# Output projection as seven products of halves, with weight sums made by adding transfers in DRAM

## The chip, the cores and the metric

The kernel runs on one core of one Trainium2 chip. The metric is the device time of one execution, in microseconds. The kernel before takes 1063.2 us (median of three runs, 1063.05 to 1063.6). A core has a matrix engine (TensorE, PE in the profile, with its weight loads as PEld), a vector engine (VectorE, DVE), a scalar engine (ScalarE, ACT), a general engine (GpSimd, POOL) and a queue engine (SyncE, SP) that here only starts transfers. Each engine works through its own instructions in order, and waits on semaphores for the others.

## The reference

One layer of an encoder block on 1024 tokens with 1024 channels, all float32:

```python
h = rms_norm(x, norm1_g)
a, gate, q, k, v = split(h @ w_in)               # 512 columns each
conv_out = silu(layer_norm(depthwise_conv_31(a * sigmoid(gate)) + bias))
q, k = rms_norm per head of 64
attn_out = neighbourhood_attention(q, k, v, rpb) # 16 rows x 64 columns of tokens, window 8 x 16
x = x + concat([conv_out, attn_out]) @ w_out     # output projection, 1024 x 1024 x 1024
h = rms_norm(x, norm2_g)                         # the second norm
x = x + (silu(h @ w_gate) * (h @ w_up)) @ w_down # 2816 hidden channels
```

## The kernel before, in words

**Precision.** Each float32 operand of a large product is split into a high part (a cast to fp32r on ACT) and a low part (the rest, a subtraction on DVE or POOL): `split`, lines L104 (cast) and L108 (subtraction). One block product is then three matmuls with 512 columns, high by high, high by low, low by high: `mac`, L112, L113, L114. Weights come by SP into raw buffers of 512 KB (three of them, pool R), and `take` splits the next one, cast on ACT, subtraction on POOL, and asks for a later one.

**Order.** The order of the work on each engine is the order in which the program issues it. Small work is put between the block products of TensorE by hand: functions are appended to the list `woven`, and `weave`, called after each `mac`, runs the next one.

**Stages.** First the k projection, the gated convolution input, the q projection (`project(0, t)`, eight token tiles) and the values (`value(t)`, eight tiles). Beside the last two run the convolution: its taps are DVE's (L319) but for some taps that ACT multiplies (L344) and POOL adds up (L345), and DVE joins the two per channel block (L324). The raw blocks of the value weights, w20 to w23, are split between the q projections. SP meanwhile builds the bias tables of the attention in DRAM (L487) and loads them (L588). Then the attention: 32 steps, each with scores (L615), a softmax whose maximum and sum run on DVE (L628) and ACT (L630) and whose scaling runs on POOL (L637), transposes (L646) and the product with the values (L662). Results of eight groups of tokens are split into high and low parts (`evac_hi` L669, `evac_lo` L674).

**Output projection.** Eight row tiles of 128 tokens by two halves of 512 output columns, each over eight blocks of 128 channels (four of the attention, four of the convolution). Column half 0 is tiles `pj`, half 1 tiles `pk`. Between the block products of `pj` lie the transposes of the convolution result (`conv_T`, L728), its statistics (`conv_stats`, L735 to L737, `conv_scale`, L747 to L756) and the transposes and silu of the normed rows (`conv_silu`, L761, L762). `resid` (L775) adds a finished tile to x on DVE.

**Second norm and gate products.** Between the block products of `pk` the rows are normed (`norm2`, L857 to L861, `norm2_out`, L867). The gate and up products, and the down product, already are made of seven products of halves each, where the four quadrants of both operands are combined by sums and differences and only seven of eight block products are made. Operands A11 and A12 are 32 transposes (`t2_one`, L994); the five others, S1 to S4 and A22, are sums of rows (`s_sum`, L944) that are transposed each by itself, 16 transposes each (`s_T`, L963), woven between the first products. Sums of the gate weights are made by `t_sums` on DVE (L893). `prep` splits the next weight operand ahead of its product, and `product` and `evac` run the products (m1 to m7) and combine their results.

**Buffers.** In SBUF 22 tiles of 4 KB per partition (G), 3 raw ones (R), 6 of 16 KB (H), 5 small ones (st). In PSUM four banks `mm`, two `tp` and one pair `cv`.

## Time and profile before

| | |
|---|---|
| median of three runs | 1063.2 us (1063.05 to 1063.6) |
| the profiled execution | 1064.03 us |
| its span, first to last instruction | 1062.2 us |
| mean granted TensorE clock | 0.999 of full speed |
| TensorE, DVE, ACT, POOL busy | 98%, 66%, 42%, 37% of the span |
| moved by transfers | 144.05 MB, 136 GB/s on average |

How to read the lines that follow: a row of the timeline has its start in microseconds from the start of the span, its length, the engine, the line of the program, the operation, output and inputs, their shapes and how many instructions are merged in it; in square brackets the idle time of the engine before it and who ended it. A row of the waits names the waiting engine and line, then whom it waited for, then the total, the number and the longest. A row of the chain of waits has a start, a length and the piece of work that the end of the run hung on. A row of the groups has the busy time in all, the mean length of one in nanoseconds and the idle time before. A row of the windows gives, for a stretch of time, the busy time of PE, PEld, DVE, ACT and POOL with the count of instructions, then the clock, the share of the transfer engines that was busy, and GB/s. Matmuls overlap, so the length of one (0.39 us) is more than the distance from one to the next.

### The profile page before, as it was taken

Reading aid. Unit: us, or ns where it says so; the run is one execution under the profiler, and the core shown is the slowest. Engines: PE = TensorE matmul, PEld = TensorE weight load, DVE = VectorE, ACT = ScalarE, POOL = GpSimd, SP = SyncE. Lnnn points to the kernel's source line nnn. Section 1 sums busy time; section 2 is a strip of 40 time slices with the busy share of each in tenths; the row PEclk is TensorE's granted clock in tenths of the full one; section 3 lists DMA queues with packets and bytes.
Section 4 is the critical chain, followed back from the end, with each engine's and each line's share of the span. In section 5 each row is a group of like instructions: output and inputs, shape, how many; then the busy total and the mean of one; then the engine's idle time right before and its main releaser. Section 6 shows DMA issues by size and latency. Waiting matters only on the chain.

```text
span 1062.2 us, 13969 instructions
## 1 busy us (share of the span) xinstructions
PE 1045.4 (98%) x5068; PEld 847.3 (80%) x5068; DVE 699.8 (66%) x1072; ACT 443.7 (42%) x874; POOL 397.3 (37%) x308
## 2 busy tenths in 40 slices
PE   7999999999999999999999999999999999999997
PEld 5788888776667888788888888888888888888886
DVE  6768998966765247666565564564655567858883
ACT  6456346626776334532323223332233344433441
POOL 0126568823542301444554544545454200002310
PEclk9999999999999999999999999999999999999999
DMA  9416681245504412032322222232132597634641
GB/s 333 164 47 225 217 257 36 75 161 154 165 34 161 136 80 99 21 129 77 136 91 104 109 99 95 104 129 100 70 131 78 194 322 276 209 99 132 205 127 43
DMA packets 68244, 144.05 MB, mean 136 GB/s; under 512 B 12496, under 2 KB 21200, under 8 KB 67536
## 3 DMA queue, kind: packets, MB, share of 16 engines
q1 hardware_dynamic: 66336, 139.95, 38.3%
q10 hardware_dynamic: 1840, 3.22, 0.9%
q8 instruction: 40, 0.66, 0.3%
q14 instruction: 28, 0.23, 0.1%
HBM read 103.99 MB, written 44.76 MB: 140 GB/s over the span
## 4 chain that ended last, share of the span: by engine, by line
PE 94%; DMA 2%; DVE 1%; ACT 1%; POOL 1%; issue 0%; SPq 0%; POOLq 0%; ACTq 0%
PE B L112 6%; PE B L114 6%; PE B L113 6%; PE A L112 4%; PE D L112 4%; PE D L114 4%; PE A L114 4%; PE D L113 4%; PE A L113 4%; PE z L113 3%; PE z L112 3%; PE z L114 3%; PE gl L114 3%; PE gl L112 3%; PE gl L113 3%; PE o L662 2%
## 5 line engine op out<-in xcount | busy, mean ns | idle before, releaser
L319 DVE SCALAR_TENSOR_TENSOR cv<-u,par,cv 128x1009 f32<-128x1009 f32 (+14 forms) x85 | 108.5, 1276 | 1.9
L345 POOL TENSOR_TENSOR pa<-pa,pr 128x1022 f32<-128x1022 f32 (+10 forms) x31 | 74.2, 2392 | 35.5 <-ACT pr L344 26.5
L104 ACT CAST op<-sr 128x512 fp32r<-128x512 f32 x77 | 47.7, 619 | 52.1 <-PE B2d L114 26.3
L108 DVE TENSOR_TENSOR op<-sr,op 128x512 fp32r<-128x512 f32 x77 | 57.1, 742 | 16.1 <-ACT op L104 16.0
L1037 DVE TENSOR_TENSOR g<-B,g 128x512 f32<-128x512 f32 x22 | 15.2, 691 | 79.0 <-PE B L114 79.0
L1209 POOL TENSOR_TENSOR ou<-ou,resm 128x512 f32<-128x512 f32 x8 | 12.2, 1530 | 144.0 <-DMA resm<-xd 142.1
L1046 ACT ACTIVATE D<-D 128x512 f32<-128x512 f32 x22 | 12.8, 582 | 113.1 <-DVE D L1045 113.1
L1032 DVE TENSOR_TENSOR u<-B,g 128x512 f32<-128x512 f32 x22 | 15.2, 691 | 62.1 <-PE B L114 62.1
L104 ACT CAST op<-wd 128x512 fp32r<-128x512 f32 x66 | 40.9, 620 | 30.7 <-DVE wd L1124 18.4
L637 POOL TENSOR_SCALAR e<-e,rs 128x288 f32<-128x288 f32 (+1 forms) x64 | 34.1, 545 | 50.2 <-DVE rs L635 42.9
L108 DVE TENSOR_TENSOR op<-wd,op 128x512 fp32r<-128x512 f32 x66 | 50.4, 764 | 1.8
L893 DVE TENSOR_TENSOR ts<-gu,ts 128x512 f32<-128x512 f32 x44 | 51.0, 1159 | 0.8
L1035 ACT ACTIVATE A<-A 128x512 f32<-128x512 f32 x20 | 11.6, 582 | 76.3 <-PE A L114 76.3
L630 ACT ACTIVATE e<-e,mx 128x288 f32<-128x288 f32 (+1 forms) x64 | 36.2, 569 | 2.0 <-DVE mx L628 2.0
L628 DVE CUSTOM_DVE_ANT_0 e<-s,tab 128x288 f32<-128x288 f32 (+1 forms) x64 | 30.1, 505 | 8.1 <-PE s L615 8.0
L344 ACT ACTIVATE pr<-u,par 128x1022 f32<-128x1022 f32 (+10 forms) x31 | 34.2, 1135 | 1.2 <-ACT vs L405 1.2
L893 DVE TENSOR_TENSOR ts<-gu 128x512 f32<-128x512 f32 x22 | 34.1, 1551 | 0.0
L646 PEld LDWEIGHTS p<-ident,e 128*96 128x96 f32 (+1 forms) x192 | 20.1, 133 | 15.2 <-issue 10.5
L944 POOL TENSOR_TENSOR xn<-xn,xn 128x512 f32<-128x512 f32 x4 | 6.9, 1732 | 57.3 <-DVE sn L944 57.3
L646 PE MATMUL p<-ident,e 128*96 128x128 f32 (+1 forms) x192 | 27.6, 280 | 0.7 <-DVE pT L651 0.6
L662 PE MATMUL o<-pT,vw 96*64 96x128 f32 (+1 forms) x384 | 28.0, 281 | 0.0
L615 PE MATMUL s<-kT,qT 64*128 64x288 f32 (+1 forms) x128 | 26.7, 495 | 0.0
(1039 smaller groups left out, 3449.6 us busy)
## 6 DMA issues: line engine op xcount, KB each, us to landing
gu<-in_gu SPq DMA_DIRECT2D x44, 512.0 KB
sr<-sd SPq DMA_DIRECT2D x77, 256.0 KB
sd<-sd SPq DMA_DIRECT2D x22, 512.0 KB
wd<-in_wd SPq DMA_DIRECT2D x44, 256.0 KB
sd<-g SPq DMA_DIRECT2D x33, 256.0 KB
x<-in_x SPq DMA_DIRECT2D x16, 512.0 KB
xd<-x SPq DMA_DIRECT2D x8, 512.0 KB
resm<-xd SPq DMA_DIRECT2D x16, 256.0 KB
```

The source lines that it names most:

```text
L104: act.copy(hi, src)
L108: eng.tensor_tensor(*[w[..., sl] for w in (lo, src, hi.bitcast(F32))], OP.subtract)
L112: pe.matmul(acc, lh, rh, start=start, stop=False, skip_group_check=True)
L113: pe.matmul(acc, lh, rl, start=False, stop=False, skip_group_check=True)
L114: pe.matmul(acc, ll, rh, start=False, stop=stop, skip_group_check=True)
L319: dve.scalar_tensor_tensor(acc[:, o], uc[:, i], dwk[:, c, t:t + 1], acc[:, o], OP.mult, OP.add)
L344: act.activation(pr[:, o], uc[:, i], AF.Copy, scale=dwk[:, c, t:t + 1])
L345: pool.tensor_tensor(pa[:, o], pa[:, o], pr[:, o], OP.add)
L630: act.activation(e[:, hh], e[:, hh], AF.Exp, bias=mx, scale=-1.0, accum_out=rs[:, hh:hh + 1])
L646: pe.transpose(pt[:m, g * P:(g + 1) * P], es[i][:, hh, g * m:(g + 1) * m], ident)
L662: pe.matmul(os_[s_][hh * HD:(hh + 1) * HD, hp], vw[cb, rh + g][:, c:c + HD], pTs[i][:, g, hh], start=g == 0, stop=g == 2)
L893: dve.tensor_tensor(o, l, r, OP.subtract)
```

## The change

**Output projection.** It becomes seven products of halves, n1 to n7, each four row tiles of 128 tokens by 512 columns over four blocks of 128 channels. The left operands are quadrants of the concatenated result and their sums: A11 (attention, second half of the tokens), A22 and A12 (convolution, first and second half), and Q1 to Q4 made of `rowf` (attention, first half) and `diff`. `evac_lo` makes A11's low part and `diff`; `conv_silu` adds to `diff` and subtracts from `rowf`. The right operands are B11, B21, B22 and the sums P1 to P4 of quadrants of the weights. n7 adds onto the banks of n1 and n5 onto those of n6. `read` adds or subtracts each finished bank to the one or two quadrants of x that it belongs to, 40 such additions of 128 x 512 in all, where `resid` made 16.

**Weight sums.** P1 to P4 are made in DRAM, beside the projections of q and the values: four plain copies on SP's queue and four transfers with addition on POOL's, each of 256 x 2048 float32 (2.10 MB). A block holds a quadrant of w_out and the same quadrant of the gate weights for the first four pairs of gate blocks, so `t_sums` is left out for these four. The order of the weight blocks to take is B11, P3, P4, P2, P1, B21, B22, two raw blocks each, 14 in place of 8.

**Second norm.** Each normed row tile is transposed once (`turn`, 8 transposes a tile, 64 in all), copied to SBUF by ACT, and the sums S1 to S4 and A22 are then made from the transposed tiles (`s_sum`, `s_split`), so that no sum is transposed.

**Gate sums.** The sums of the gate weights are additions, and the signs move into the evacuations, which subtract. The products of the first four gate blocks run in another order, m1 and m2 of all four first.

The core of the diff (`T_`, `C`, `QS`, `N`, `U`, `SS` and `SP` only wrap `conv_stats`, `conv_silu`, `q_split`, `norm2_out`, `turn`, `s_sum` and `s_split` for weaving):

```diff
+    order = [m + h * FB // 2 for m in range(FB // 2) for h in range(2)]
+    gs = gu[order[:4]].reshape(4, 2, P, 2, 512)
+    wq = f["w_out"].reshape(2, 2, 2, P, 2, 512)[::-1].transpose(0, 4, 1, 3, 2, 5)
+    w4 = np.stack([np.concatenate([wq[k, d].ravel(), gs[:, d, :, k].ravel()]) for k in range(2) for d in range(2)])
...
-    wo, woq = {}, {}
-
-    def wo_dst(d, k0):
+    BLK = {"B11": 0, "B12": 1, "B21": 2, "B22": 3}
+    pw = {n: dr.tile([256, 2048], F32, name=n) for n in ("P1", "P2", "P3", "P4")}
+    wq = {}
+
+    def block(n):
+        return a["w4"][BLK[n]] if n in BLK else pw[n]
+
+    def sum_steps():
+        def copy(n, m):
+            return lambda: nc.sync.dma_start(pw[n], block(m))
+
+        def add(n, m):
+            return lambda: pool.dma_start(pw[n], block(m), accum_op=OP.add, max_dma_last_dim=2048)
+        return [[copy("P1", "B12"), copy("P3", "B12")], [], [add("P1", "B11"), add("P3", "B22")], [],
+                [copy("P2", "P1")], [], [add("P2", "B22")], [], [copy("P4", "P2")], [], [add("P4", "B21")]]
+
+    def wq_dst(n, j):
         def dst():
-            if (d, k0 // 4) not in woq:
-                woq[d, k0 // 4] = H(f"wo{d}{k0}", F32R)
-            q = woq[d, k0 // 4]
-            o = k0 % 4 * 1024
-            hl = (q[:, o:o + 1024], q[:, o + 1024:o + 2048])
-            for j in range(2):
-                wo[d, k0 + j] = [w[:, j * 512:(j + 1) * 512] for w in hl]
-            return hl
+            if j == 0:
+                wq[n] = H(f"w{n}", F32R)
+            return [wq[n][:, o + j * 1024:o + j * 1024 + 1024] for o in (0, 2048)]
         return dst
 
-    for d in range(2):
-        for k0 in (4, 6, 0, 2):
-            want(a["wo"][k0 * P:(k0 + 2) * P, d * 512:(d + 1) * 512].rearrange("(k p) m -> p k m", p=P),
-                 f"wo{d}{k0}", wo_dst(d, k0), (pool,) * 4 if d == 0 and k0 < 4 else (pool,))
+    for n in ("B11", "P3", "P4", "P2", "P1", "B21", "B22"):
+        for j in range(2):
+            want(block(n)[64 * j:64 * j + 64].rearrange("r (h e) -> (r h) e", h=2), f"{n}{j}", wq_dst(n, j))
 
 
...
+    steps = sum_steps()
+
+    def aside_sum():
+        for f in steps.pop(0) if steps else ():
+            f()
+
     for t in range(8):
         project(0, t, head_post)
+        aside_sum()
         if t % 2 == 0:
             take()
...
+            if not rowf:
+                rowf.extend(G(f"rf{j}").rearrange("p (c b q) -> p c b q", c=2, b=4) for j in range(2))
+            for j in range(2):
+                act.copy(rowf[j][:, :, cb], os_[s_][:, 2 * j:2 * j + 2])
+        else:
+            a11[cb] = [w.rearrange("p (c q) -> p c q", c=4) for w in lr(G(f"a11{cb}", F32R))]
+            act.copy(a11[cb][0], os_[s_])
+
+    def evac_lo(s_, js=(0, 1)):
         rh, cb = order[s_]
-        hi, lo = [w[:, cs, rh] for w in at[cb]]
-        dve.tensor_tensor(lo, os_[s_][:, cs], hi.bitcast(F32), OP.subtract)
+        if rh == 0:
+            return
+        if not diff:
+            diff.extend(G(f"df{j}").rearrange("p (c b q) -> p c b q", c=2, b=4) for j in range(2))
+        for j in js:
+            cs = slice(2 * j, 2 * j + 2)
+            hi, lo = [w[:, cs] for w in a11[cb]]
+            dve.tensor_tensor(lo, os_[s_][:, cs], hi.bitcast(F32), OP.subtract)
+            dve.tensor_tensor(diff[j][:, :, cb], os_[s_][:, cs], rowf[j][:, :, cb], OP.subtract)
 
     def value(t):
+        aside_sum()
...
+    def lhs(p, c, cb):
+        if p == "n1":
+            return [w[:, c] for w in a11[cb]]
+        q, o = qop[LHS[p]], c * 512 + cb * P
+        return [q[:, o:o + P], q[:, 2048 + o:2048 + o + P]]
+
+    LHS = {"n7": "Q3", "n4": "A22", "n6": "Q2", "n5": "Q1", "n2": "A12", "n3": "Q4"}
+    RHS = {"n1": "B11", "n7": "P3", "n4": "P4", "n6": "P2", "n5": "P1", "n2": "B21", "n3": "B22"}
+    CB = (0, 3, 1, 2)
+
+    def proj(p, cb, acc, cs=range(4), start=True):
+        w = wq[RHS[p]]
+        for c in cs:
+            mac(acc, lhs(p, c, cb), [w[:, o + c * 512:o + c * 512 + 512] for o in (0, 2048)],
+                start and c == 0, c == 3)
             weave()
 
+    def q_split(n, f, j, eng):
+        if j == 0:
+            qop[n] = H(n, F32R)
+        split(*[qop[n][:, o + j * 1024:o + j * 1024 + 1024] for o in (0, 2048)],
+              f[j].rearrange("p c b q -> p (c b q)"), (eng,))
+
...
+        n = ("A22", "A12")[h]
+        if c == 0:
+            qop[n] = H(n, F32R)
+        tiles = lambda w: w.rearrange("p (b i j) -> p i b j", b=4, j=16)
+        hi, lo = [tiles(qop[n][:, o + c * 512:o + c * 512 + 512]) for o in (0, 2048)]
+        y4 = y.rearrange("p (i b j) -> p i b j", b=4, j=16)
+        split(hi, lo, y4, (dve,))
+        d, r = [tiles(w[c // 2][:, c % 2].rearrange("p b q -> p (b q)")) for w in (diff, rowf)]
+        dve.tensor_tensor(d, y4, d, OP.subtract if h else OP.add)
+        if h == 0:
+            dve.tensor_tensor(r, r, y4, OP.subtract)
 
...
+    def read(p, cb):
+        acc = pb[cb]
+        if p == "n1":
+            put(4 + cb, 0, acc)
+            put(4 + cb, 1, acc, OP.subtract)
+        elif p == "n7":
+            put(cb, 1, acc, OP.subtract)
+            put(cb, 0, acc)
+        elif p in ("n4", "n6"):
+            put(cb, 0, acc, OP.add if p == "n4" else OP.subtract)
+        elif p == "n5":
+            put(cb, 1, acc)
+            put(4 + cb, 1, acc)
+            norm2(cb)
+        elif p == "n2":
+            put(4 + cb, 0, acc)
+        else:
+            put(4 + cb, 1, acc)
+            norm2(4 + cb)
 
...
+    SRC = {"m6": "P2", "m5": "P1", "m7": "P3", "m3": "B22", "m4": "P4"}
+    firsts = [(i, None) for i in range(4)] + [(p, pr) for pr in range(2) for p in SRC]
+    queue = firsts + [(i, j) for i in range(4, FB) for j in range(2)]
+
+    def next_raw():
+        if queue:
+            n, j = key = queue.pop(0)
+            raws2[key] = R(f"gu{n}{j}")
+            if n in SRC:
+                src = block(SRC[n])[128 + 64 * j:192 + 64 * j].rearrange("(i r) (h e) -> (r h) i e", i=2, h=4)
+                nc.sync.dma_start(raws2[key].rearrange("p (i e) -> p i e", i=2), src)
+            else:
+                nc.sync.dma_start(raws2[key], a["gu"][ms[n], j or 0])
 
...
-            o = lr(tsum[i, (n - 1) // 2])[(n - 1) % 2]
-            l, r = ((b12, b11), (b22, lr(tsum[i, 0])[0]), (b22, b12), (b21, lr(tsum[i, 0])[1]))[n - 1]
-            dve.tensor_tensor(o, l, r, OP.subtract)
+            p1, p2 = lr(tsum[i, 0])
+            o, l, r = ((p1, b11, b12), (p2, p1, b22), (None, b12, b22), (None, p2, b21))[n - 1]
+            dve.tensor_tensor(lr(tsum[i, 1])[n - 3] if o is None else o, l, r, OP.add)
...
+    products = [(i, p) for k in (0, 2) for p in ("m1", "m2") for i in (k, k + 1)]
+    products += [(i, p) for k in (0, 2) for p in SRC for i in (k, k + 1)]
+    products += [(i, p) for i in range(4, FB) for p in ORDER]
...
+    def turn(t, j):
+        if not h2:
+            h2.extend(H(f"h2{w}", F32R).rearrange("p (k s) -> p k s", s=512) for w in range(2))
+        pt = tp(f"t2{t}{j}")
+        for i in range(4):
+            kb = 4 * j + i
+            pe.transpose(pt[:, i * P:(i + 1) * P], xn[t][:, kb * P:(kb + 1) * P], ident)
+        if j == 0:
+            xT[t] = G(f"xT{t}")
+        w = lr(xT[t])[j]
+        if t < 4:
+            hi, lo = [q[:, 4 * j:4 * j + 4, t * P:(t + 1) * P] for q in h2]
+            p3 = pt.rearrange("p (k s) -> p k s", s=P)
+            act.copy(hi, p3)
+            act.copy(w, pt)
+            rest.append(lambda: dve.tensor_tensor(lo, p3, hi.bitcast(F32), OP.subtract))
         else:
+            act.copy(w, pt)
...
+    def group(p, cbs=CB):
+        for cb in cbs:
+            more = p in ("n7", "n5")
+            if not more:
+                pb[cb] = mm(f"{p}{cb}")
+            proj(p, cb, pb[cb], start=not more)
+            read(p, cb)
+
+    for cb in CB:
+        load_x2(4 + cb)
+    conv_stats(0, conv_T(0))
+    weaves(12, s0=lambda: (weigh(31), evac_hi(7), evac_lo(7)), s1=T_(1), s2=T_(2), s3=[T_(3), lambda: read("n1", 0)],
+           s4=QS("Q3", diff, 0, pool), s5=T_(4), s6=take, s7=T_(5), s8=QS("Q3", diff, 1, pool), s9=T_(6), s10=take, s11=T_(7))
+    group("n1", CB[1:])
+    for cb in CB:
+        load_x2(cb)
+    act.activation(warm, eps, AF.Silu)
+    weaves(16, s1=C(0, 0), s3=take, s4=C(0, 1), s7=C(0, 2), s9=QS("Q2", diff, 0, pool), s10=C(0, 3), s11=take, s13=C(1, 0),
+           s15=QS("Q2", diff, 1, pool))
+    group("n7")
+    weaves(16, s0=C(1, 1), s2=take, s3=C(1, 2), s6=C(1, 3), s8=QS("Q1", rowf, 0, pool), s10=take, s11=QS("Q1", rowf, 1, dve))
+    group("n4")
+    weaves(16, s0=take, s1=QS("Q4", diff, 0, dve), s4=QS("Q4", diff, 1, pool), s6=take)
+    group("n6")
+    weaves(16, s1=take, s6=take, s9=N(0), s13=N(3))
+    group("n5")
+    for _ in range(3):
+        next_raw()
+    weaves(16, s0=take, s1=[N(1), U(0, 0)], s2=U(0, 1), s3=[lo2, lo2], s4=U(3, 0), s5=[U(3, 1), N(2)], s6=[lo2, lo2],
+           s7=U(1, 0), s8=U(1, 1), s9=[lo2, lo2, prep], s10=[U(2, 0), take], s11=U(2, 1), s12=[lo2, lo2], s13=prep)
+    group("n2")
+    weaves(16, s3=prep, s7=prep, s9=N(4), s12=U(4, 0), s13=[U(4, 1), N(7)], s15=SS(0, 1, 2))
+    group("n3")
     sop["A11"], sop["A12"] = ([[w[:, o + k] for k in range(HK)] for w in h2] for o in (0, HK))
+    plan = {
+        0: dict(s0=U(7, 0), s1=[U(7, 1), N(5)], s2=SP("S2", 0), s3=SS(3, 1, 2)),
+        1: dict(s0=U(5, 0), s1=[U(5, 1), N(6)], s2=SP("S2", 3), s3=SS(1, 1, 2)),
+        2: dict(s0=U(6, 0), s1=[U(6, 1), lambda: act.activation(warm, eps, AF.Silu)], s2=SP("S2", 1), s3=SS(2, 1, 2)),
+        3: dict(s0=SP("S2", 2), s2=SP("S1", 0), s3=SP("S1", 3)),
+        4: dict(s0=SP("S1", 1), s1=SP("S1", 2), s2=SS(0, 3), s3=SS(3, 3)),
+        5: dict(s0=SS(1, 3), s1=SS(2, 3), s2=SS(0, 4, eng=pool), s3=SS(3, 4, eng=pool)),
+        6: dict(s0=SS(1, 4, eng=pool), s1=SS(2, 4, eng=pool), s3=SP("S3", 0)),
+        7: dict(s1=SP("S3", 3), s3=SP("S3", 1)),
+        8: dict(s1=SP("S3", 2)),
+        9: dict(s1=SP("S4", 0), s3=SP("S4", 1)),
+        10: dict(s1=SP("S4", 2)),
+        11: dict(s1=SP("S4", 3)),
+        12: dict(s1=SP("A22", 0), s3=SP("A22", 1)),
+        13: dict(s1=SP("A22", 2), s3=SP("A22", 3)),
+    }
 
...
-            dve.tensor_tensor(u2[i], acc, l, OP.add)
+            dve.tensor_tensor(u2[i], acc, l, OP.subtract)
```

269 lines of the change are left out of this document (101 added, 168 removed).

## The prediction

> **What bounds the kernel now.** I read the page first, then the waits of TensorE, its groups and pace, and the order in time of the other engines around the places that the change touches.
>
> ```profile
> span 1062.2 us, 13969 instructions
> PE 1045.4 (98%) x5068; PEld 847.3 (80%) x5068; DVE 699.8 (66%) x1072; ACT 443.7 (42%) x874; POOL 397.3 (37%) x308
> GB/s 333 164 47 225 217 257 36 75 161 154 165 34 161 136 80 99 21 129 77 136 91 104 109 99 95 104 129 100 70 131 78 194 322 276 209 99 132 205 127 43
> ```
>
> TensorE is busy nearly throughout. Its waits, longest first, leave little to win by waiting less:
>
> ```profile
> PE z L113 <- POOL w23l L108: 0.7, 1, 0.7
> ...
> PE t L994 <- DVE xn L867: 0.6, 1, 0.6
> ...
> PE B L113 <- DVE S L108: 0.3, 1, 0.3
> ```
>
> So the time changes by the TensorE instructions that go and by the new waits on TensorE. The pace of a 512-column matmul comes from the timeline: 24 of them (one z tile) lie between these two starts, (151.31 - 145.87) / 24 = 0.2267 us each. Four transposes take 0.44 us in the chain of waits, eight take 0.87, so 0.109 us each.
>
> ```profile
> 145.87 0.39 PE L112 MATMUL z<-w00h,hT 128*128 128x512 f32 x1
> ...
> 151.31 0.39 PE L112 MATMUL z<-w00h,hT 128*128 128x512 f32 x1
> ```
> ```profile
> 241.05 0.81 PE p L646 x6
> ...
> 317.91 0.44 PE y L728 x4
> ...
> 442.24 0.87 PE sp L963 x8
> ```
>
> **What goes.** The output projection has 8 row tiles x 2 column halves x 8 blocks x 3 matmuls = 384; seven products of halves have 7 x 4 tiles x 4 blocks x 3 = 336. 48 x 0.2267 = **10.9 us**. The transposes of the second norm are 32 (L994) and 80 (L963, five operands of 16); afterwards each of 64 blocks is turned once. 48 x 0.109 = **5.3 us**. The two small waits at these transposes (0.6 + 0.3 = **0.9 us**) belong to work that goes. Together 17.1 us.
>
> ```profile
> L994 PE MATMUL t<-ident,xn 128*128 128x128 f32 x32 | 5.0, 274 | 0.6 <-DVE xn L867 0.6
> ```
>
> **Weight sums in DRAM.** Four copies on SP's queue and four adding transfers on POOL's, 2.10 MB each, go out one group at a time after the q projections 0, 2, 4, 6 and values 0 and 2. They pass through two queues that other work needs.
>
> ```profile
> 171.30 2.40 POOL L108 TENSOR_TENSOR w21l<-w21r,w21h 128x1024 fp32r<-128x1024 f32 x1
> ...
> 179.07 2.39 POOL L345 TENSOR_TENSOR pa<-pa,pr 128x1015 f32<-128x1015 f32 x1 [0.56 <-ACT pr L344]
> ...
> 184.78 4.88 POOL L345 TENSOR_TENSOR pa<-pa,pr 128x1022 f32<-128x1022 f32 x2 [0.93 <-ACT pr L344]
> 190.78 4.87 POOL L345 TENSOR_TENSOR pa<-pa,pr 128x1020 f32<-128x1020 f32 x2 [1.12 <-ACT pr L344]
> 195.59 2.40 POOL L108 TENSOR_TENSOR w23l<-w23r,w23h 128x1024 fp32r<-128x1024 f32 x1
> ...
> 208.97 7.29 POOL L345 TENSOR_TENSOR pa<-pa,pr 128x1014 f32<-128x1014 f32 x3 [0.52 <-ACT pr L344]
> 231.38 0.99 POOL L637 TENSOR_SCALAR e<-e,rs 128x288 f32<-128x288 f32 x2 [15.11 <-DVE rs L635]
> ```
> ```profile
> 151.83 0.53 SPq L141 DMA_DIRECT2D w22r<-in_qkv  x1
> ...
> 192.36 24.99 SPq L588 DMA_DIRECT2D tab<-tf  x5
> ```
> ```profile
> 198.05 0.50 PE z L113
> ```
>
> The adds into P1 and P3 stand before w21l on POOL, the add into P2 before w23l, and w23l already ends last at the wait at 198.05. POOL's gaps between them (0.56 + 0.93 + 1.12 = 2.6 us) take up the first two. No POOL-issued transfer is in this trace, so the price of issuing one lies between SP's 0.53 us and POOL's longest single instruction, 2.40; I take 1.2, nearer to the SP row, since both only start a transfer. Two (2.4) fit the gaps, the third is paid: 1.2. For the wait of the second add on the copy before it I add 0.8: both copies go out just ahead of w22r (151.83) and carry 4.19 MB, which takes 12.6 us at the page's best 333 GB/s or 16.8 at the 249 of their own window, until about 173. Sum **2.0 us** (range 0 to 5).
>
> ```profile
> 150.00:160.00 10.00, 10.00 (x46) 8.29 (x45) 9.75 (x12) 4.35 (x5) 4.48 (x3) 1.00 0.85 249
> ```
>
> How long an add takes, call it a, is not in the trace either. From below 2.10 MB / 333 = 6.3 us; from above three passes (two reads, one write) at 249, 25.3. I take 12.6, two passes at 333: nearest is the plain copy, and the add reads twice what a copy reads. POOL issues the first adds at 172.5. With adds in order, P1 is done at 172.5 + a, its copy into P2 (8 us) at 180.5 + a, and POOL comes to the add into P2 at 198: no stall up to a = 17.5. Three adds, the copy into P4 (8), the last issue (1.2) and two late side taps (4.8) must end by 236, which is DVE's last conv sum at 228.15 plus 8 of the 8.7 us between the end of POOL's first pass over the softmax (231.38 + 0.99) and the transposes at 241.05 that want it: 172.5 + 3a + 14 = 236 gives a = 16.5. The bias tables (192.36) wait on SP behind the copy into P4, with about the same bound. At 12.6 the cover holds and the chain costs nothing; beyond 16.5 each microsecond costs three.
>
> ```profile
> 204.42 23.63 DVE L319 SCALAR_TENSOR_TENSOR cv<-u,par,cv 128x1009 f32<-128x1009 f32 x18
> 228.15 1.22 DVE L324 TENSOR_TENSOR u<-cv,pa 128x1024 f32<-128x1024 f32 x1
> ```
>
> The Trainium skill, "DMA: Bandwidth & Descriptors", section "Anatomy of one DMA — SWDGE (gpsimd) path", fits such a transfer by 2.0 us plus bytes over 436 GB/s, 6.8 us as an estimate here; no run here shows it yet, it was fitted without addition, and by it the sum stays the same.
>
> **Attention loop.** The subtractions of evac_lo now fall in every other group, four instead of two of 0.41 us. An iteration lasts 2.46 us, of which DVE is busy 7.55 tenths, so it has 0.6 us of slack; two doubled groups in a row (0.82 more) just pass it, four times in the loop: **0.5 us** (0 to 1).
>
> ```profile
> 306.69 0.84 PE s L615 x4
> ...
> 309.15 0.84 PE s L615 x4
> ```
> ```profile
> 300.00:310.00 10.00, 10.00 (x91) 6.37 (x90) 7.55 (x26) 8.01 (x26) 6.05 (x11) 1.00 0.02 6
> ```
>
> **The first product (n1) and the change to the second (n7).** Here I expect the dear part. n1 has 12 slots of 0.68 us after its first tile, in which all 8 conv statistics, two takes of P3, two splits of Q3 and eight additions into x2 must pass; before, 20 slots held the statistics.
>
> ```profile
> 311.88 0.41 DVE L674 TENSOR_TENSOR at<-o,at 128x256 fp32r<-128x256 f32 x1
> ...
> 323.13 0.70 DVE L735 BATCH_NORM_STATS2 bs<-y 128x6 f32<-128x512 f32 x1 [0.29 <-PE y L728]
> ...
> 324.14 0.16 DVE L755 SCALAR_TENSOR_TENSOR bb<-bm,br 128x1 f32<-128x1 f32 x1
> ...
> 327.72 0.60 DVE L755 SCALAR_TENSOR_TENSOR bb<-bm,br 128x1 f32<-128x1 f32 x1
> ...
> 352.52 2.47 DVE L775 TENSOR_TENSOR x<-pj,x 128x512 f32<-128x512 f32 x4
> ```
> ```profile
> 322.69 0.29 ACT L737 ACTIVATE bd<-bm,eps 128x1 f32<-128x1 f32 x1 [1.64 <-DVE br L747]
> 322.94 0.78 ACT L756 ACTIVATE xh<-y,bb,br 128x512 f32<-128x512 f32 x1
> ...
> 325.07 1.04 ACT L104 CAST wo<-wo02r 128x1024 fp32r<-128x1024 f32 x1
> ```
> ```profile
> 355.29 2.40 POOL L108 TENSOR_TENSOR wo<-wo16r,wo 128x1024 fp32r<-128x1024 f32 x1
> ```
>
> On the clock of before, TensorE would end n1 at 317.9 + 12 x 0.68 + 8 x 0.44 + 0.81 = 330.4. DVE: the last evac_lo (4 x 0.41) to 322.3; statistics 1 to 3, some 1.15 each (323.13 to the end of bb at 324.30), to 325.7; additions for two tiles (4 x 0.62) to 328.1; statistics 4 to about 329.9. ACT follows in order: scales 1 and 2, the first cast of Q3 (1.04) to 327.4, then root 4, scales 3 and 4, and the first cast of P3 to 331.8. POOL subtracts 2.40 each: Q3 half 0 to 329.8, P3 half 0 from 331.8 to 334.2, Q3 half 1 to 336.6, P3 half 1 to 339.0. TensorE needs P3's low parts at 330.4 (half 0) and two blocks and four transposes later (half 1): it waits until 334.2 and again until 339.0, when without waits it would be at 330.4 + 1.36 + 0.44 = 332.2. That is 6.8 us. DVE adds to it where POOL holds it:
>
> ```profile
> 172.21 1.52 DVE L383 TENSOR_SCALAR r<-r,r 128x8 f32<-128x8 f32 x1
> ...
> 178.88 0.23 DVE L383 TENSOR_SCALAR r<-r,r 128x8 f32<-128x8 f32 x1
> ```
>
> The same small instruction takes 0.23 us, or 1.52 when POOL's w21l (171.30 to 173.70) runs: it ends with it. The statistics' bb shows the same, 0.16 and 0.60, the latter beside POOL pieces of 0.7 us. The new POOL pieces are 2.40 whole. One such hold at statistics 5 (up to 2.4, 1.2 of it reaching the last cast) makes **8.0 us**, range 3 to 12; zero if TensorE's wait is shorter because ACT and POOL run ahead of DVE. The Trainium skill, "SBUF — State Buffer", section "Who interferes with whom", has the rule: DVE with two SBUF inputs contends with a POOL instruction that reads SBUF, and the first issued keeps the ports. The rows agree; without it the term would be 6.8.
>
> **Behind it.** By the same accounting n4, n6 and n5 find their operands ready: DVE's lag of about 5 us is worked off in n4 and n6, where it has some 8 and 4 us of work in 12 and 11. In n2, eight turns with two ACT copies each fill ACT; one turn waits 0.6 us for its bank: **0.6** (0 to 2). The products after that, with spread splits and four fewer gate sums, have cover: operand S2 is wanted eight products (22 us) after its first rows. Add against subtract costs nothing, one instruction for one. Loads: the projection takes 14 raw blocks of 512 KB in place of 8, the first four gate products 14 in place of 8. On SP the x2 loads for n7 now stand behind a raw block that waits for P3's split (334.2), and land some 3 us later than that, ahead of the additions of n7 (past 341); the gate blocks are asked for at least two products (5.4 us) ahead. These cost nothing while their order holds; an x2 load that came late would hold DVE, and with it n4's banks.
>
> **Sum.** -17.1 + 2.0 + 0.5 + 8.0 + 0.6 = -6.0 us. The profiled execution took 1064.03 us (span 1062.2 and 1.8 around it), the median is 1063.2, 0.8 lower: 1064.0 - 6.0 - 0.8 = **1057.2 us**.
>
> **Rivals.** (A) The covers hold everywhere: TensorE stays gapless and the full 17.1 us come out, 1064.0 - 17.1 - 0.8 = 1046.1. For it: POOL is empty from 330 to 340 before, and the first product's work may be issued earlier than my order in time has it. Against: eight additions, four more POOL passes and the statistics in 12 slots instead of 20. (B) Slower: the chain of transfers in DRAM holds POOL. If an add takes 21 us, near to three passes, POOL blocks in front of w23l and the side taps, SP in front of the bias tables, and the attention starts 3 x (21 - 16.5) = 13.5 us late: 1070.7. From a = 19 on it is slower than before. For it: DRAM traffic at 249 GB/s, ten passes of 2.10 MB; against: the page shows 36 and 75 GB/s in the two slices from 159 on, so the transfers are alone. (C) DVE doesn't catch up after n7: every hold by POOL costs its whole 2.4 us and the waits repeat at n4 and n6, three of them, 7.2 us more: 1064.4. For it: DVE has 17 us of work in n1 against TensorE's 12, and 15 against 13 in n7; against: the work falls behind them.
>
> ```profile
> 330.00:340.00 10.00, 9.98 (x50) 7.76 (x51) 4.63 (x11) 4.90 (x9) 0.00 (x0) 1.00 0.62 215
> ```
>
> **Chances.** Forecast 0.52 (own range 1051 to 1061, from the 0 to 5 and 3 to 12 above), A 0.20, B 0.16, C 0.12. A measurement of this kernel can tell 0.2%, 2.1 us, from no change. Faster: forecast, A and 0.04 of C, 0.76; same: 0.03 of C and 0.01 of B, 0.04; slower: 0.15 of B and 0.05 of C, 0.20. The range reaches A's value below and past C above, leaving out most of B and what lies under A: 1046 to 1068.
>
> **What would show it.** Right: TensorE has 96 instructions fewer between 311 and 460; its list of waits names a POOL low part of P3 or Q3 with some 6 to 8 us, and POOL subtracts without a pause around 331 to 339; w23l ends 1 to 3 us late. Wrong: no TensorE wait over 1 us (A); waits on w23l, on the tables or a late start of the attention beyond 245 (B); waits in n4 or n6 on DVE's additions (C).

## The result: 1.3% slower, and the profile after

The changed kernel takes 1077.84 us (median, 1076.27 to 1078.15), the kernel before 1063.4 beside it: a ratio of 1.0131, 95% interval 1.0113 to 1.0148. The forecast was 1057.2 us in a range of 1046 to 1068, so sign and range were both wrong. The profiled execution of the changed kernel took 1076.27 us.

The page of the changed kernel, its span and the engines' busy time:

```profile
span 1074.5 us, 13918 instructions
...
PE 1038.4 (97%) x4972; PEld 840.0 (78%) x4972; DVE 732.8 (68%) x1094; ACT 466.4 (43%) x913; POOL 444.8 (41%) x326
```

TensorE has 4972 instructions against 5068: the 96 that should go are gone. What came in their place is in its list of waits (engine and line, whom it waited for, total, number, longest):

```profile
PE zt L407 <- DVE zn L400: 7.2, 2, 5.5
...
PE y L785 <- ACT xh L813: 4.3, 2, 4.1
PE n L120 <- POOL wP L115: 2.5, 2, 2.0
PE z L120 <- POOL w23l L115: 1.9, 1, 1.9
PE z L818 <- DVE df L828: 1.7, 1, 1.7
PE t L1019 <- DVE h L1028: 1.5, 2, 1.2
PE t L1019 <- DVE xn L915: 1.2, 1, 1.2
PE B L121 <- POOL t0m L115: 1.1, 1, 1.1
PE B L119 <- DVE u L1141: 0.8, 1, 0.8
```

Before, no wait was over 0.7 us but that for the very first weights. The new ones fall into two groups: zt and w23l lie in the chain of the q heads, the others behind the attention. The first matmul of the output projection starts at 311.54 us before and at 322.67 after; from there to the end of the span it is 750.66 and 751.83 us. So the changed kernel loses 11.1 us ahead of the projection, and behind it, where most of the 17.1 us should have come out, it takes 1.2 us more than before.

**Ahead of the projection.** Timelines of the changed kernel: DVE's multiplication of the norm factor r of a head, the value that zn and then TensorE's transposes zt wait for, and POOL at those times.

```profile
171.04 6.55 DVE L398 TENSOR_SCALAR r<-r,r 128x8 f32<-128x8 f32 x1
...
202.13 5.05 DVE L398 TENSOR_SCALAR r<-r,r 128x8 f32<-128x8 f32 x1
```
```profile
170.11 2.81 POOL L206 DMA_DIRECT2D P<-in_w  x2
171.92 3.37 POOL L115 TENSOR_TENSOR w21l<-w21r,w21h 128x1024 fp32r<-128x1024 f32 x1
174.25 3.31 POOL L360 TENSOR_TENSOR pa<-pa,pr 128x1017 f32<-128x1017 f32 x1
...
177.64 2.34 POOL L360 TENSOR_TENSOR pa<-pa,pr 128x1016 f32<-128x1016 f32 x1
...
224.55 1.29 POOL L206 DMA_DIRECT2D P<-in_w  x1 [2.03 <-DMA P<-P]
```

An instruction of eight elements a partition takes 6.55 and 5.05 us instead of 0.23. Look at POOL's ends: behind the issues (to 172.92) w21l begins 1.0 us before they end, and the next sum (174.25) 1.0 us before w21l ends (175.29). The first place where POOL's instructions don't overlap is between 177.56 (174.25 + 3.31) and 177.64, and there r ends: 171.04 + 6.55 = 177.59. The second hold ends in the same way: 202.13 + 5.05 = 207.18, and POOL's first boundary without an overlap is between 207.15 and 207.22. In the kernel before, w21l ends at 173.70 beside r's 173.73, and nothing there overlapped by more than 0.04.

TensorE then pays twice, by the wait and by its clock:

```profile
178.47 1.08 PE L407 MATMUL zt<-ident,zn 128*128 128x128 f32 x4 [5.46 <-DVE zn L400]
...
180.21 0.63 PE L121 MATMUL z<-w00h,hT 128*128 128x512 f32 x1
...
182.32 0.40 PE L120 MATMUL z<-w01l,hT 128*128 128x512 f32 x1
```
```profile
170.00:180.00 10.00, 4.54 (x20) 3.62 (x19) 9.90 (x6) 2.53 (x5) 9.90 (x6) 0.77 0.88 161
...
200.00:210.00 10.00, 6.33 (x26) 4.70 (x25) 9.63 (x7) 3.22 (x7) 9.49 (x5) 0.81 0.93 162
...
340.00:350.00 10.00, 7.75 (x35) 6.34 (x35) 6.64 (x15) 5.67 (x9) 5.52 (x4) 0.83 0.20 69
...
460.00:470.00 10.00, 8.09 (x28) 5.93 (x27) 9.03 (x10) 6.57 (x13) 10.00 (x8) 0.83 0.31 105
```

From 180.21 to 182.32 five matmuls take 0.42 us each instead of 0.2267. The windows (busy time of PE, PEld, DVE, ACT, POOL, then the granted clock) show 0.77 and 0.81 here, and 0.83 in two stretches behind the attention. The Trainium skill, "TensorE: Matmul & The Clock Gate", Part 1, says that the clock falls to half after an idle window of about 3.4 us and returns after as much activity. After the wait of 5.46 us the trace agrees: the distance of the matmuls nearly doubles for some 3.9 us.

**Behind it**, the longest wait of the changed kernel, by the timelines of TensorE, ACT, DVE and POOL:

```profile
342.25 0.73 PE L785 MATMUL y<-ident,u 128*128 128x128 f32 x4 [4.08 <-ACT xh L813]
```
```profile
340.74 1.45 ACT L813 ACTIVATE xh<-y,bb,br 128x512 f32<-128x512 f32 x2 [0.76 <-DVE br L804]
```
```profile
336.30 2.47 DVE L842 TENSOR_TENSOR x<-x,n 128x512 f32<-128x512 f32 x4
...
339.68 0.97 DVE L812 SCALAR_TENSOR_TENSOR bb<-bm,br 128x1 f32<-128x1 f32 x1
```
```profile
338.29 2.34 POOL L115 TENSOR_TENSOR Q<-df,Q 128x1024 fp32r<-128x1024 f32 x1 [13.04 <-ACT Q L111]
```

In `four`, two of every four tiles share a pair of banks, a half each, and the other two get a bank of their own. The transposes here are tile 5's. They write the second half of the pair whose first half holds tile 4, and `conv_stats` issues the scaling of tile 4, which reads that half, ahead of them; so they wait until it ends (342.19). The scaling waits for DVE, which does four additions into x first (2.47 us) and whose bb of the tile before is then held for 0.97 by POOL's Q. POOL in turn had been idle for 13.04 us.

### The profile page after: what moved, and what is told of

Read it like the earlier page. It is cut to its first block, busy times and chain, and to the rows that moved or that the text cites. A ratio compares the mean times of both kernels' runs of the same rounds, so it can differ in the third digit from the quotient of the medians.

```text
span 1074.5 us, 13918 instructions
## 1 busy us (share of the span) xinstructions
PE 1038.4 (97%) x4972; PEld 840.0 (78%) x4972; DVE 732.8 (68%) x1094; ACT 466.4 (43%) x913; POOL 444.8 (41%) x326
## 4 chain that ended last, share of the span: by engine, by line
PE 84%; issue 6%; POOL 4%; DVE 3%; DMA 2%; ACT 1%; SPq 0%; POOLq 0%; ACTq 0%; DVEq 0%
PE B L121 5%; PE B L120 5%; PE B L119 5%; PE D L120 4%; PE D L121 4%; PE D L119 4%; PE z L119 3%; PE z L121 3%; PE z L120 3%; PE A L120 3%; PE A L121 3%; PE A L119 3%; PE gl L121 3%; PE gl L119 3%; PE gl L120 3%
## 5 line engine op out<-in xcount | busy, mean ns | idle before, releaser
L1314 POOL TENSOR_TENSOR ou<-ou,resm 128x512 f32<-128x512 f32 x8 | 12.6, 1590 | 142.3 <-DMA resm<-xd 142.3
L941 DVE TENSOR_TENSOR ts<-ts,gu 128x512 f32<-128x512 f32 x36 | 43.3, 1203 | 0.6
L842 DVE TENSOR_TENSOR x<-x,n 128x512 f32<-128x512 f32 x40 | 26.1, 680 | 13.0 <-PE n L121 13.0
L941 DVE TENSOR_TENSOR ts<-gu 128x512 f32<-128x512 f32 x18 | 30.2, 1680 | 0.0
(1056 smaller groups left out, 3527.5 us busy)
```

Source lines behind the costliest of these rows:

```text
L941: dve.tensor_tensor(lr(tsum[i, 1])[n - 3] if o is None else o, l, r, OP.add)
```

## The experiments

All times are medians beside the kernel before on the same chip (1063.2 to 1063.6).

**The sums alone.** Into the kernel before go the four copies and four additions, at the same places; nothing reads P1 to P4.

```diff
     for t in range(8):
         project(0, t, head_post)
+        aside_sum()
...
     def value(t):
+        aside_sum()
```

> The kernel before with the four copies and four adding transfers of the change put in at the same places; their results are not used. Theory H (hold): on POOL the issue of an adding transfer and the additions that stand right behind it leave no gap for DVE's small product r times r1 in the head scale, which needs two operands from SBUF; TensorE waits for its result twice, about 5.5 us each, and comes back at a lower clock. H expects both waits here too, the attention 10 to 12 us later than before, 1073 to 1076 us. Rival T (traffic): the bytes cost, by late loads; the waits of TensorE would name a transfer. The recorded prediction had 2 us for this part: 1065.4.

1076.59 us, ratio 1.0123 (1.0108 to 1.0138). Waits and DVE's timeline of this kernel:

```profile
PE zt L412 <- DVE zn L405: 7.3, 2, 5.5
```
```profile
172.16 6.58 DVE L403 TENSOR_SCALAR r<-r,r 128x8 f32<-128x8 f32 x1
...
203.94 5.05 DVE L403 TENSOR_SCALAR r<-r,r 128x8 f32<-128x8 f32 x1
```

13.0 us, with the same holds, from transfers whose results nobody uses; the attention starts at 240.84 us in place of 227.56.

**Without the additions.** The changed kernel with the copies but no additions (so P1 to P4 lack their second summand):

```diff
-        return [..., [], [add("P1", "B11"), add("P3", "B22")], ..., [add("P2", "B22")], ..., [add("P4", "B21")]]
+        return [..., [], [], ..., [], ..., []]
```

> The changed kernel without the four adding transfers; the copies stay, so the weight sums lack their second summand. H: the early stage returns to that of before, the attention starts 10 to 12 us earlier than in the changed kernel, 1065 to 1068 us. T: the copies are 8.4 of the 16.8 MB that the eight transfers carry, so half of the loss stays: about 1072.

1063.44 us, ratio 1.000 (0.9991 to 1.001). That is below both expectations. The additions cost 1077.84 - 1063.44 = 14.4 us; the rest of the change, in its order, is worth nothing. Its waits behind the attention are nearly those of the changed kernel:

```profile
PE y L785 <- ACT xh L813: 4.3, 2, 4.1
PE n L120 <- POOL wP L115: 1.9, 2, 1.4
```

**Traffic or issue?** The additions cover 16 of the 256 rows of 2048 (not 16 of each 512 x 512 block, as the expectation has it):

```diff
-            return lambda: pool.dma_start(pw[n], block(m), accum_op=OP.add, max_dma_last_dim=2048)
+            return lambda: pool.dma_start(pw[n][:16], block(m)[:16], accum_op=OP.add, max_dma_last_dim=2048)
```

> Edit: the four transfers with addition cover only the first 16 rows of each 512x512 block; the sums are left without their second summand beyond those rows. Theory 1 (the instructions by which POOL issues the additions, 1.3 us each with casts back to back behind them, are what holds the two-operand multiplication r on DVE): the holds of 6.55 and 5.05 us stay, PE still waits some 7 us for zn in all, and the time stays near the changed kernel's, 1073 to 1077 us. Theory 2 (the 19.0 us that each addition's data travels is the loss: traffic on the engines that move data, and POOL's next step waiting for it): both go, and the time is near that without additions, 1063 to 1065 us. In between, some 1068 us, if the first hold goes and the second stays.

1073.37 us, ratio 1.0084 (1.0067 to 1.0101). DVE's timeline, and the time from issue to landing of the additions:

```profile
171.20 5.57 DVE L398 TENSOR_SCALAR r<-r,r 128x8 f32<-128x8 f32 x1
...
201.09 4.56 DVE L398 TENSOR_SCALAR r<-r,r 128x8 f32<-128x8 f32 x1
```
```profile
DMA to landing us min/median/max: 3.1/3.6/3.8
```

They land in 3.6 us and r is still held, here too until the first place between POOL's instructions without an overlap (176.72 to 176.80; r ends at 176.77): the hold comes with the issue on POOL and the casts and sums behind it, not with the data. 9.9 of the 14.4 us stay.

**r on another engine.** The multiplication r of the q heads goes to ACT:

```diff
+        if n == 0:
+            act.activation(r, r, AF.Copy, scale=r1[:, t:t + 1])
+        else:
             dve.tensor_scalar(r, r, r1[:, t:t + 1], None, op0=OP.mult)
```

> The changed kernel with the product r times r1 of the q heads made on ACT in place of DVE; all transfers stay. H: the two waits on DVE's zn go, w23l's wait of 2 us may stay, 1066 to 1069 us. T: no change, 1077 to 1078.

1075.69 us, ratio 1.0117 (1.0101 to 1.0133). Waits, and the addition into P2 on POOL:

```profile
PE z L120 <- POOL w23l L115: 4.4, 1, 4.4
...
PE o L687 <- DMA vw<-vd: 2.6, 1, 2.6
```
```profile
198.40 1.27 POOL L206 DMA_DIRECT2D P<-in_w  x1 [0.69 <-DMA P<-P]
```

The waits for zn fall from 7.2 to 0.4 us, as expected, but the time misses the expected 1066 to 1069 us: only 2 us come back. The move itself costs nothing that shows: from the first to the sixth head's transposes zt it is 30.28 us, against 30.22 in the kernel without additions, which has r on DVE. What the hold had hidden is the next bound, w23l behind the additions in POOL's queue, and SP's queue:

```profile
216.16 0.50 SPq L203 DMA_DIRECT2D P<-P  x1
216.83 7.13 SPq L613 DMA_DIRECT2D tab<-tf  x5
```

The attention's tables stand behind the copy into P4, which waits for the addition into P2; without additions they start at 191.46. The first rows of vw, behind the tables, are asked for at 227.25 instead of 216.57, and from the third group of scores to the projection it takes 75.57 us instead of 71.24. So the losses don't add up: without the hold the additions still cost 12.3 us (1075.69 - 1063.44), and with hardly any data 9.9.

**The additions somewhere else.** First in the gate stage (copies from 21.7 us on, additions from 37.6), where POOL had little to do:

```diff
-        return [[copy("P1", "B12"), copy("P3", "B12")], [], [add("P1", "B11"), add("P3", "B22")], ...]
+        return {1: [copy("P1", "B12"), copy("P3", "B12")], 3: [add("P1", "B11"), add("P3", "B22")],
+                8: [copy("P2", "P1")], 11: [add("P2", "B22")], 15: [copy("P4", "P2")], 18: [add("P4", "B21")]}
```

> Edit: the copies and additions are issued while the gate stage's first products run (from about 40 us), where POOL and the transfers have little else, and not in the chain of heads. Theory (the place of the additions is what costs the 12 to 14 us, since they meet POOL's casts and DVE's r there): r takes 0.23 us in the head chain, the waits for zn of 7.2 us go, the attention starts some 12 us earlier, and the time is that of the kernel without additions, 1063 to 1065 us, with all four sums made. Rival (adding in DRAM costs wherever it lies, because it takes transfers from the loads of inputs or POOL from the gate): the loss only moves, and the time stays over 1071 us.

1094.05 us, ratio 1.0283 (1.0268 to 1.0299), against the expectation:

```profile
PE z L119 <- ACT w02h L111: 12.1, 1, 12.1
PE z L120 <- POOL w00l L115: 7.6, 1, 7.6
```
```profile
150.23 1.29 POOL L206 DMA_DIRECT2D P<-in_w  x1 [15.96 <-DMA tf<-t]
```

No wait for zn is over 0.4 us, which fits the theory of the hold. But SP's queue builds the bias tables here, and beside the additions they take longer (ten transfers in 15.27 us from 99.76, in 7.11 without additions). So w02r behind them is asked for at 162.1 us instead of 131.4, and POOL stands 15.96 us before the addition into P4, with w00l behind it.

Then late, in the value steps and the attention, with P2 and P4 begun from inputs so that no copy waits for an addition:

```diff
+        return {0: [copy("P1", "B12"), copy("P3", "B12")], 4: [copy("P2", "B22")], 6: [copy("P4", "B21")],
+                9: [add("P1", "B11")], 11: [add("P3", "B22")], 15: [add("P2", "P1")], 16: [add("P4", "P2")]}
```

> Edit: the four additions are issued one by one while DVE's small multiplication r no longer stands between TensorE and its next transposes: P1 and P3 in the second and fourth value step, P2 in the last, P4 in the attention; P2 and P4 begin as copies of inputs, so that no copy waits for an addition. Theory (what the additions cost is only where POOL's issue and the casts right behind it fall: on r of the head chain): r takes 0.23 us everywhere, no wait for zn, the attention starts within 1 us of the kernel without additions (226.7 us), and the time is 1063 to 1065 us with all sums made. Rival (the additions cost wherever they lie, as in the gate stage, by keeping the transfers of the attention's rows or POOL's divisions waiting): waits for vw or pT of over 5 us in all and a time over 1068 us.

1084.76 us, ratio 1.0211 (1.0194 to 1.0228): the rival.

```profile
PE o L685 <- DMA vw<-vd: 9.9, 3, 6.0
...
PE p L669 <- DVE pT L674: 4.8, 3, 2.9
```
```profile
231.55 1.27 POOL L206 DMA_DIRECT2D P<-P  x1 [14.59 <-DMA P<-in_w]
```

The attention starts on time (226.10 us against 226.65 without additions), but POOL stands 14.6 us behind P1, and vw's rows come late: from the third group of scores to the projection it takes 92.18 us instead of 71.24.

**The late stage.** One edit first: the scaling is issued one tile later.

```diff
-        if 1 <= t <= 4:
+        if t:
             conv_scale(t - 1)
-        if t >= 4:
-            conv_scale(t)
+        if t == 7:
+            conv_scale(7)
```

> The changed kernel with the scaling of each convolution tile issued one tile later throughout (before, tiles 4 to 7 were scaled at once). Theory P (pair): the wait of 4.1 us in n1 is for the scaling of tile 4, which reads the other half of the bank pair that the transposes of tile 5 write; issued behind these transposes it no longer holds them, the wait goes with the low clock after it, 1072 to 1075 us. Rival D (DVE): DVE is late anyway, and the wait moves to the transposes of tile 6 or 7: 1076 to 1078.

1075.37 us, ratio 1.0109 (1.0094 to 1.0124), 2.5 us less. The wait for xh falls from 4.3 to 0.2 us; y now waits 1.3 us for DVE's statistics bs, and n 3.9 instead of 2.5 for wP. Two more edits were added to this one, over the sums in the gate stage: first a bank per tile, out of three, then P3's takes and Q3's subtractions earlier.

```diff
-        wide.append(lr(cv(name)) if n % 4 == 0 else wide[n - 1] if n % 4 == 1 else None)
-        return wide[n][n % 4] if n % 4 < 2 else tp(name)
+        wide.append(None)
+        return cv(name)[:, :512] if n % 3 == 0 else tp(name)
```
```diff
+    take()
-    weaves(12, ..., s4=QS("Q3", diff, 0, pool), ..., s6=take, ..., s8=QS("Q3", diff, 1, pool), ..., s10=take, ...)
+    weaves(12, ..., s1=[T_(1), take], s2=[T_(2), QS("Q3", diff, 0, pool)], ..., s4=QS("Q3", diff, 1, pool), ...)
```

> Edit: as with the sums made early, and in the transposes of the second norm's rows the scaling is issued one tile later and each tile gets a bank of its own out of three, where two tiles share one pair of banks in the changed kernel. Theory (the pair of banks, given back only once its two tiles are scaled, is what the 4.3 us for xh and the 1.7 us for df are due to, and TensorE's low clock after them adds some 4 us): both waits go, and the time is 4 to 7 us below that of the sums made early: 1057 to 1060 us. Rival (the additions of the rows on DVE are the bound there, so waits move from xh to bs or n): the waits of this stage add up to over 4 us again and the time is within 2.5 us of the sums made early.

> Edit: as with the separate banks, and in the last products of the convolution the half sums of the combined weights P3 are taken one or two steps earlier, and the differences of Q3 are issued on POOL two and four steps in, where they start four and eight steps in in the changed kernel. Theory (n waits 2.5 us for wP and t for xn and h, because POOL begins Q3 only after 13 us idle and its casts queue behind the scales): n's wait for wP goes and the time falls another 2 to 4 us, to 1054 to 1058 us, below the kernel before. Rival (POOL's earlier differences hold DVE's additions in the same steps): n's wait goes but y or bs waits as long, and the time stays that of the separate banks or rises.

1088.15 us with the later scaling and the banks (5.9 less than 1094.05; n's wait for wP grew from 1.7 to 3.5 us) and 1085.61 with the order too (2.5 less again; that wait fell to 0.5). The same three edits without additions separate the two losses:

> Edit: the kernel without additions (so P1 to P4 lack their second summand) with the three edits of the late stage. It was at 1063.4 us, 14.4 below the changed kernel. Theory (the late loss is the change's own order of banks and of POOL's halves, whatever happens before): 8 us less, 1054 to 1057 us, which is what the change is worth once both its losses but the rest of the late waits are gone. Rival (the late loss follows from the time shift of the transfers before it): under 4 us less, 1060 us or more.

1055.58 us, ratio 0.9923 (0.9908 to 0.9938), 7.9 less than without them. So these 7.9 us of the late loss come from the change's own order, whatever the additions do. Waits behind the attention:

```profile
PE y L785 <- ACT xh L813: 1.6, 4, 0.5
PE t L1019 <- DVE h L1028: 1.5, 2, 1.1
```

Over the sums issued late the three edits gave 1077.14 us (7.6 less). A fourth, POOL's subtractions for S4 two to four products earlier, made it 1079.31: t0m's wait went, one of 3.1 us for u came, and pT's in the attention grew from 3.3 to 9.0 us, where nothing had been edited. So how much of the 2.2 us S4 is to blame for stays open.

> Edit: as with the sums issued late, and the three edits of the second norm and convolution as in the run of the earlier order (scaling one tile later, a bank for each tile, halves of P3 and Q3 earlier). With the sums early these three brought 1094.05 to 1085.61 us, 8.4 us. Theory (early and late losses have nothing to do with each other): 1064 - 8.4, so 1054 to 1057 us, faster than the kernel before. Rival (the late stage gains only because its transfers and POOL's work were out of phase with the long waits before it): less than 4 us below the sums issued late.

> Edit: as with the late sums and the earlier order, and the eight subtractions that POOL makes for S4 are issued in the second to fifth product of the gate sums, where POOL has some 6 of 10 us free, in place of the sixth and seventh, where it and the casts for t0m and t1m run back to back for 25 us. Theory (the wait for t0m of 1.1 us, that for u of 0.8 and the TensorE clock of 0.83 in those 10 us come from POOL's backlog): those waits go, and the time falls by 2 to 4 us against the late sums and earlier order. Rival (POOL's subtractions hold DVE's sums of the same steps, which S2 and S1 wait for): waits for S or sn appear at the products that use them and the time does not fall.

**All sums made, and no loss against the kernel before.** r on ACT, P2 and P4 begun from inputs, one addition every second head; then with the three late edits:

```diff
+        return {0: [copy("P1", "B12"), copy("P3", "B12")], 1: [copy("P2", "B22")], 3: [copy("P4", "B21")],
+                2: [add("P1", "B11")], 4: [add("P3", "B22")], 6: [add("P2", "P1")], 9: [add("P4", "P2")]}
```

> Edit: r of the heads on ScalarE as in that run, P2 begins as a copy of B22 and P4 as one of B21 (from the inputs, early), and the four additions are issued one at a time in every second head, so that no copy and no addition stands in the queue behind an unfinished one. Theory (with the hold gone, the chain of copies is the bound: w23l's wait of 4.4 us and the vw wait of 2.6): both waits go, the attention starts within 2 us of the kernel without additions, and the time is 1063 to 1066 us. Rival (the traffic of 8.4 MB is the bound itself, so it only keeps others waiting): the weights of the heads or vw come late again, over 3 us in all, and the time stays over 1070 us.

> Edit: head_sums together with the three edits of the late stage (scaling one tile later, a bank for each tile, halves of P3 and Q3 earlier), which brought 8.4 us with the sums in the gate stage and 7.6 with them issued late. Theory (early and late losses are separate): 8 us below head_sums, so 1055 to 1058 us if that is at 1063 to 1066. Rival (as before, a chain of transfers elsewhere decides): as head_sums, less than 5 us below it.

1071.06 us, ratio 1.0069 (1.0054 to 1.0084), and 1063.79, ratio 1.0003 (0.9993 to 1.0013). Vw's wait is gone, w23l's is 6.5 and 5.3 us: the addition into P2 stands ahead of w23l and waits for P1. The last two move it behind w23l and P1 one head earlier:

```diff
+        return {0: [copy("P1", "B12"), copy("P3", "B12")], 1: [copy("P2", "B22"), add("P1", "B11")],
+                3: [copy("P4", "B21"), add("P3", "B22")], 7: [add("P2", "P1")], 11: [add("P4", "P2")]}
```

> Edit: as head_order, with the addition P1 one head earlier, P2 behind POOL's cast of w23 in place of ahead of it, P4 two slots later, P3 one head earlier. Theory (only a place in POOL's queue behind an unfinished addition costs, since r is on ScalarE): w23l's wait falls from 5.3 to under 2 us, the attention starts 226.5 to 229 us in, and the time is 1056 to 1060 us, 4 to 7 below the kernel before. Rival (the traffic decides): w23l comes as late through its transfer, or vw's rows wait over 3 us, and the time stays at 1062 to 1066.

> Edit: as best_a, with the addition P3 behind P2 in place of two heads after P1, so that POOL issues only one addition while its casts and products run without a gap. Theory: as best_a, 1056 to 1060 us, and less of the first heads' waits if any are left. Rival (P3 beside P4 keeps the attention's first rows of vw waiting, as the sums issued late did): waits for vw over 3 us and a time of 1062 us or more.

The first takes 1061.58 us, ratio 0.9981 (0.997 to 0.9992): 2 us less than the kernel before and 16 less than the changed one, but short of the expected 1056 to 1060. The second, with P3's addition behind P2's, takes 1066.29 (1.0025, 1.0016 to 1.0033), vw's rows being 6.1 us late. What is left in the first, by its waits and POOL's timeline:

```profile
PE z L120 <- POOL w23l L115: 2.3, 1, 2.3
PE s L641 <- DVE mx L654: 2.2, 1, 2.2
```
```profile
233.12 1.29 POOL L206 DMA_DIRECT2D P<-P  x1 [16.82 <-DMA P<-P]
```

That leaves 6.0 us between the best order found and the kernel whose sums are not completed (1055.58), and no run shows an order that makes the additions for nothing.

## Why the prediction was wrong, point by point

- **What goes, 17.1 us.** The counts were right (96 instructions, two small waits).
- **Weight sums, 2.0 us: the step that failed.** It measured 13.0 us in the kernel before and 14.4 in the changed one. The prediction priced POOL's issue (1.2, measured 1.26 to 1.79) and the wait of POOL for a copy (0.8; by its own figures the copies end at 151.83 + 16.8 = 168.6, and POOL waits for none at 170.11), and asked who else waits in POOL's and SP's queues. It did not ask whom POOL holds while it works without a pause. The row for that was quoted, r at 172.21 with 1.52 instead of 0.23 us, but used only for n1. And an issue was taken to cost its own time only ("take up the first two" gaps): behind it POOL's next instructions overlap in the record, and the hold, which the first boundary ended before, runs on over several of them. The clock after each wait, not priced either, adds to it: against the kernel without additions the projection starts 12.05 us later, and the waits for zn and w23l grow by 8.0. The length of an addition, next, is the second half of the error; the run with r on ACT shows that mending the hold alone gives 2 us.
- **Length of an addition, a = 12.6 us.** It lands after 19.0 us here (14.1 to 31.5), nearer to the upper bound (25.3) than to the lower (6.3):

```profile
P<-in_w POOLq DMA_DIRECT2D x4, 2048.0 KB, 19.0
```

  By the fit of the Trainium skill, "DMA: Bandwidth & Descriptors", that the prediction cited it would be 6.8, an estimate; addition in DRAM took nearly three times that, and the page names no addition beside its fit. The cover's limit of 16.5 is thus passed. In the changed kernel POOL waited only 2.03 us, since everything was late already; with r on ACT the limit shows. **Rival B** named this chain (POOL in front of w23l, SP in front of the tables) and, from a = 19 on, a time slower than before. Its sign came true, and its chain stands right behind the hold; the hold, which ends last in the changed kernel, it doesn't have.
- **Attention loop, 0.5 us.** From the third group of scores to the projection it is 71.25 us before and 71.24 after: nothing.
- **n1 and n7, 8.0 us.** The waits of y, n and z make 4.3 + 2.5 + 1.7 = 8.5 us, close to 8.0 by luck, since they lie on another path and in part further on. The prediction put the wait on POOL's low parts of P3, 6.8; that is 2.0 (the other 0.5 of n's wait is in n6). It did not follow the banks, where transposes wait for work on the tile in the other half of their pair: 4.1 in n1, and 1.7 in n4. Nor did it price the clock: it is 0.83 in the ten microseconds from 340.
- **Turns in n2, 0.6; gate products, 0.** The waits on h and xn make 2.7, those on t0m and u 1.9, with the clock low again. "Have cover" was said of DVE's splits; the engine without cover is POOL: 10.00 busy of 10 in the window from 460, quoted above.
- **Together.** From the attention on, 0.5 + 8.0 + 0.6 = 9.1 us of the 17.1 were expected to be lost; without additions the stretch from the projection to the end is 750.28 us against 750.66, so 16.7 were lost, of which the three edits return 7.9. What goes did go: with these edits TensorE is busy for 727.7 us of that stretch instead of 743.1, but idle for 14.6 instead of 7.4. Forecast and measurement differ by 20.6 us: about 12.4 from the additions (14.4 instead of 2.0), 7.6 from the late stage, the rest from rounding and the chip.
- **Rival A** (1046.1) is not reached by any run; 1055.58 is the nearest. **Rival C** (DVE doesn't catch up) came in a small way, once, with 1.7 us instead of three times 2.4. The wait is in n4, on DVE's addition into `diff`, which reads the other half of the bank pair; DVE had additions into x ahead of it:

```profile
367.75 0.63 PE L818 MATMUL z<-ident,xh 128*128 128x128 f32 x4 [1.74 <-DVE df L828]
```

## What to carry to other kernels

Before moving work to an engine, ask not only who is queued behind it but whom it holds while it runs; a row where a small instruction takes several times its usual length is a price that can come back multiplied. A transfer that nobody waits for still has a place: four additions of the same size cost 6 to 31 us by their place and by what stood beside them, each time through another neighbour. Two bounds of like length hide each other: taking one away gave 2 of 14 us. And a new wait is priced by its length plus the clock after it, and looked for in the banks as well as in the engines' orders.

## What the runs showed of the hardware that was not expected

- A DVE instruction with two operands in SBUF was held for 6.55 us (0.23 alone), over two issues and two instructions of POOL, up to the first boundary between them without an overlap; before it the record shows overlaps of 0.5 to 1.0 us. That the overlap is the cause is argued from the ends of four such rows, not shown by a run. The Trainium skill, "SBUF — State Buffer", section "Who interferes with whom", has the contention of the two engines and lets the first to issue keep the ports for its whole instruction; here the hold goes on into the next ones.
- A transfer with addition of 2.10 MB between DRAM tensors landed after 19.0 us in the median, and after 25.7 to 34.9 (medians) in the four kernels that spread the additions over the heads; why longer there was not settled.
- The distance of TensorE's matmuls grew to 0.43 us also after waits of 0.81 and 1.10 us that began only 1.5 us apart, with two matmuls between them (they ended at 463.25 and 465.06 in the changed kernel). Each is far below the idle window of 3.4 us in the Trainium skill, "TensorE: Matmul & The Clock Gate", Part 1:

```profile
463.25 0.47 PE L119 MATMUL B<-S,t0m 128*128 128x512 f32 x1 [0.81 <-DVE u L1141]
...
465.06 0.50 PE L121 MATMUL B<-S,t0m 128*128 128x512 f32 x1 [1.10 <-POOL t0m L115]
...
466.07 0.63 PE L121 MATMUL B<-S,t0m 128*128 128x512 f32 x1
466.50 0.63 PE L119 MATMUL B<-S,t0m 128*128 128x512 f32 x1
```
